# A full-height tile for the low part of q in the attention scores of a four-mixer decoder layer

## The chip, the cores and the metric

The kernel runs on one core of one Trainium2 chip. The metric is the device time of one execution in microseconds (us), start to end. Engines: TensorE (PE, with its weight load shown apart as PEld), VectorE (DVE), ScalarE (ACT), GpSimd (POOL) and SyncE (SP), which issues the DMAs here.

## The reference, cut to what matters

One layer (`DEPTH = 1`) over 1024 tokens of width 1024. After an RMSNorm, one input projection feeds four token mixers; their outputs are normalised per head, gated, concatenated and sent through one output projection. Three of the mixers are causal attentions with 64-wide queries and keys; the fourth (D) is a recurrence.

```python
proj = h @ w_in[l]
...
s = jnp.einsum('bhqcd,bhkcd->bhcqk', qb, k).astype(jnp.float32) * scale + bias[None, :, None]   # A
w = p[:, :, 0] - lam * p[:, :, 1]
...
z = jnp.einsum('bhqd,bhkd->bhqk', qb, k).astype(jnp.float32) * scale                            # B
a = jnp.where(causal, jnp.exp(log_beta + after), 0.0)
...
s = jnp.einsum('bhqd,bhkd->bhqk', qb, k).astype(jnp.float32) * scale                            # C
s = s + (fb[..., :, None] - cum_f[..., None, :])
...
h_res = h_res + mixed @ w_out[l]
```

All of it is in float32, so products that matter are made from operands split in two parts, a high one rounded for the matmul and a low one that holds the rest.

## The kernel before, in words

**Stages.** First the norm, then group D's projections and preparation. Then twelve attention jobs in a row (line 1076): jobs 0 to 3 are pairs of heads of B, jobs 4 to 7 heads of A (two score maps each), jobs 8 to 11 pairs of heads of C. While job i is computed, the projections of job i + 1 and some gate projections are computed too: their matmuls (line 280, in `proj`) stand between the attention matmuls on PE. GpSimd splits every projection weight into `wh` and `wl` (lines 191 and 192 in `load_w`), and, spread over jobs 0 to 3 by a low priority, it inverts group D's triangles (`inv_steps`, lines 855 and 857). After job 11 come group D's chunk chain (`chunk_local`, `chunk_state`, whose matmuls are in `four`, line 968) and the output projection (`out_blocks`, line 931). The output weights are split by `split_w`: seven of the sixteen 128-row blocks early, into tiles that the attention gives back (`split_w_early`), nine later (`split_w_late`).

**Order.** The program is written as one stream; a scheduler puts it into a fixed order on each engine when the kernel is built, and each engine runs its own list in that order. The only fixed order between engines is by semaphores.

**The scores.** Two 64-row heads (or the two maps of one A head) share a job's tiles. `proj_qk` makes from a projection of 128 rows (head 0 on partitions 0 to 63, head 1 on 64 to 127) the tiles `q0`, `q1` and `ql`, one for each half of the tokens, and `k0`, `k1`. In `k0` partitions 0 to 63 hold the high part of head 0's keys and 64 to 127 the low part; in `k1` it is the other way round for head 1. `q0` holds the high part of head 0's queries twice, `q1` that of head 1. `ql` holds the low part of both heads' queries, each on its own 64 partitions. So in `scores` the first matmul gives high times high plus high times low over 128 rows, and the second adds low times high over the 64 rows of its head:

```python
n = h * 64
mm = nc.tensor.matmul(ps[:, :w], lhsT=t[f"q{h}"][qh][:, qs], rhs=t[f"k{h}"][:, c0:c1], start=True, stop=False)
nc.tensor.matmul(ps[:, :w], lhsT=t["ql"][qh][n:n + 64, qs], rhs=t[f"k{h}"][n:n + 64, c0:c1], start=False, stop=not diag)
```

The first is line 397, the second line 401; line 403 adds a mask, in B alone. Each job calls `scores` 24 times, 288 in all. The columns `w` are 128 to 512: a block of 128 queries against the keys up to its own, in chunks of at most 512. In `proj_qk` line 323 makes the low part, `ql` for queries and `kl` for keys. The attention's own tiles lie in the pool `attw`; `q0`, `q1`, `ql` have three buffers each.

Of the kernel before, what the change touches and what calls it, by code (L numbers as in the profile page):

```python
# [10 lines left out]
F32 = mybir.dt.float32  # L11
F32R = mybir.dt.float32r
# [3 lines left out]
ALU = mybir.AluOpType  # L16
# [3 lines left out]
P = 128  # L20
# [3 lines left out]
HS = 512  # L24
# [31 lines left out]
WORDER = (4, 5, 6, 7, 8, 9, 0, 1, 10, 11, 2, 3, 12, 13, 14, 15)  # L56
# [34 lines left out]
def hybrid_trunk_kernel(  # L91
# [23 lines left out]
    nc = tc.nc  # L115
# [3 lines left out]
    def pool(stack, name, bufs=1, space=None, side="left"):  # L119
        kw = {"side": side, "reuse_waits": "tile"} if space is None else {"space": space}  # L120
        return stack.enter_context(tc.tile_pool(name=name, bufs=bufs, **kw))
# [5 lines left out]
    def bank(tag, bufs, name):  # L127
        return psum.tile([P, HS], F32, tag=tag, bufs=bufs, name=name)
# [3 lines left out]
    def rdma(dst, src):  # L132
        nc.sync.dma_start(dst.bitcast(F32), src.bitcast(F32))
# [28 lines left out]

    exp_ln_tables()

# [1 line left out]
    cst = cp.tile([P, C_END], F32, name="cst")  # L166
    def vec(src, n, name, eng=nc.sync):
        t = cp.tile([P, n], F32, name=name)
# [61 lines left out]
    nc.vector.tensor_scalar(qkg[:, 0:1], qkg[:, 0:1], 0.125, None, op0=ALU.mult)  # L230
    nc.vector.tensor_scalar(qkg[:, 2:3], qkg[:, 2:3], 0.125, None, op0=ALU.mult)

# [1 line left out]
    hTh = hpool.tile([P, KT, S], F32R, name="hTh")  # L234
    hTl = hpool.tile([P, KT, S], F32R, name="hTl")

# [6 lines left out]
    with xst:  # L243
# [14 lines left out]
        for hf in range(2):  # L258
            for kt in range(KT):
                ps = bank(("pj", "sc", "mm")[kt % 3] if hf == 0 else ("sc", "mm")[kt % 2], 2, "pst")  # L260
# [4 lines left out]
                split = nc.scalar.activation(dh, ps, AF.Copy, scale=ng[:, kt:kt + 1])  # L265
# [1 line left out]
                    after(split, norms[ACTORD[kt]])  # L267
                nc.vector.scalar_tensor_tensor(dl, ps, ng[:, kt:kt + 1], dh.bitcast(F32), op0=ALU.mult, op1=ALU.subtract)  # L268

# [1 line left out]
    def proj(col, evac, M=P, hold=None, wts=None):  # L271
        wts = load_w(col) if wts is None else wts
        pss = [bank("pj", 2, "pj") for _ in range(2)]
        for hf in range(2):
            cs = slice(hf * HS, (hf + 1) * HS)
            n = 0
            for kt in range(KT):
                wh, wl = wts[kt // 4]
                for a, b in ((wh, hTh), (wh, hTl), (wl, hTh)):
                    mm = nc.tensor.matmul(pss[hf][:M, :], lhsT=a[:, kt % 4, :M], rhs=b[:, kt, cs], start=n == 0, stop=n == 3 * KT - 1)  # L280
                    if n == 0 and hold is not None:
                        after(mm, hold)
                    n += 1
            evac(hf, cs, pss[hf])

# [1 line left out]
    class Att:  # L287
        pass

    at = Att()  # L290
    at.held = []

    def head_rstd(src, sumw, width, sq, ps, table=None):
        nc.scalar.activation(sq, src, AF.Square)
        nc.tensor.matmul(ps, lhsT=sumw, rhs=sq, start=True, stop=True)  # L295
        rstd_from(sq, ps, 1.0 / width, eps, table)
        return sq

    def qk_tiles(pl):
        t = {}  # L300
        for n in ("q0", "q1", "ql"):
            t[n] = [pl.tile([P, HS], F32R, tag=n, bufs=3, name=n) for _ in range(2)]
        for n in ("k0", "k1"):
            t[n] = pl.tile([P, S], F32R, tag=n, bufs=2, name=n)
        return t

    late_qk = dram.tile([4, P, HS], F32, name="late_qk")

    def proj_qk(col, which, t, gain, tmp, late=None):
        def finish_qk(hf, cs, ps, table=None):  # L310
            a0, a1 = t[which + "0"], t[which + "1"]
            if which == "q":
                a0, a1, cs = a0[hf], a1[hf], slice(0, HS)
            low = t["ql"][hf] if which == "q" else tmp.tile([P, HS], F32R, tag="pjl", bufs=1, name="kl")
            if gain is None:
                src, sc = ps, (0.125 if which == "q" else 1.0)
            else:
                src, sc = tmp.tile([P, HS], F32, tag="pjt", bufs=2, name="qn"), 1.0
                rs = head_rstd(ps, blk, 64, src, bank("pn", 1, "psn"), table)
                nc.vector.scalar_tensor_tensor(src, ps, gain, rs, op0=ALU.mult, op1=ALU.mult)  # L320
            nc.scalar.activation(a0[:, cs], src, AF.Copy, scale=sc)
            nc.scalar.activation(a1[:, cs], src, AF.Copy, scale=sc)
            nc.vector.scalar_tensor_tensor(low, src, sc, a0[:, cs].bitcast(F32), op0=ALU.mult, op1=ALU.subtract)
            if which == "q":
                rdma(a0[64:128, cs], a1[0:64, cs])
                rdma(a1[0:64, cs], a1[64:128, cs])
            else:
                rdma(a0[64:128, cs], low[0:64])
                rdma(a1[0:64, cs], low[64:128])

        def evac(hf, cs, ps):
            if late is None:
                finish_qk(hf, cs, ps)
                return
            raw = tmp.tile([P, HS], F32, tag="pjt", bufs=2, name="qr")
            nc.scalar.copy(raw, ps)
            spot = late_qk[2 * (which == "k") + hf]
            nc.sync.dma_start(spot, raw)

            def finish_late(table):  # L340
                src = at.fin.tile([P, HS], F32, tag="gl", bufs=2, name="ql")
                nc.sync.dma_start(src, spot)
                finish_qk(hf, cs, src, table)

            late.append(finish_late)

        proj(col, evac)
# [43 lines left out]
    def scores(t, h, qb, c0, c1, last=None):  # L391
        ps = bank("sc", 2, "sc")
        w = c1 - c0
        qs = slice(qb % 4 * P, qb % 4 * P + P)
        qh = qb // 4
        n = h * 64
        mm = nc.tensor.matmul(ps[:, :w], lhsT=t[f"q{h}"][qh][:, qs], rhs=t[f"k{h}"][:, c0:c1], start=True, stop=False)  # L397
        if at.first is None:
            at.first = mm
        diag = last is not None and c1 == (qb + 1) * P  # L400
        nc.tensor.matmul(ps[:, :w], lhsT=t["ql"][qh][n:n + 64, qs], rhs=t[f"k{h}"][n:n + 64, c0:c1], start=False, stop=not diag)  # L401
        if diag:
            nc.tensor.matmul(ps[:, w - P:w], lhsT=identb, rhs=last, start=False, stop=True)
        return ps
# [41 lines left out]
        nc.gpsimd.tensor_mul(y, y, gt)  # L446
        nc.sync.dma_start(mix[f * P:f * P + P, cs], y)

# [1 line left out]
    def proj_pair_b(p, pl, tmp):  # L450
        t = qk_tiles(pl)
        proj_qk(COL["bq"] + p * P, "q", t, None, tmp)
# [43 lines left out]
        else:  # L496
            finish(ot, f, J, blk, 64, tmp)

# [1 line left out]
    def setup_a(tmp):  # L500
        oht = tmp.tile([NB, OHW], F32, tag="oh", bufs=1, name="oht")
        nc.sync.dma_start(oht, onehot)
# [76 lines left out]
            else:  # L579
                finish(ot, p, J, ones, 128, tmp)  # L580

# [1 line left out]
    at.fbt = cp.tile([72, 1], F32, name="fbt")  # L583
    after(nc.sync.dma_start(at.fbt[64:72, :], forget_bias.rearrange("o h -> h o")), w_dma[-1])
    at.fb = at.fbt[64:72]
# [45 lines left out]
            else:  # L631
                finish(ot, 8 + p, J, blk, 64, tmp)

# [1 line left out]
    rw = Att()  # L635

    def spill(name):
# [201 lines left out]
                nc.scalar.copy(dst[64 * h:64 * h + 64, :, c2, :], src[64 * c2:64 * c2 + 64, :, h, :])  # L839
        keep(rw.rkv, 2, vt)  # L840

# [1 line left out]
    def inv_load(ip):  # L843
        rw.y = ip.tile([P, CH, CH], F32, name="yinv")
        rw.ytmp = ip.tile([P, 512], F32, name="ytmp")
# [14 lines left out]
        for q in range(4):  # L860
            nc.sync.dma_start(rw.abky[:, :, 3, q].rearrange("c (h t) s -> (c h) t s", h=2), rw.y[32 * q:32 * q + 32])

# [1 line left out]
    def split_w(f, opr, wh, wl):  # L864
        raw = opr.tile([P, DM], F32, tag="raw", bufs=2, name="wraw")
        nc.sync.dma_start(raw, w_out[0, f * P:(f + 1) * P, :])
# [14 lines left out]
    def wide(pl, tag, name):  # L881
        return [pl.tile([P, DM], F32R, tag=tag, bufs=2, name=name)]

    def thin(pl, tags, name):
        return [pl.tile([P, HS], F32R, tag=t, bufs=3, name=name) for t in tags]

    def split_w_early(pl, opr, wo):
        def vs_pair(f):
            t = pl.tile([P, 2, DM], F32R, tag="vs", bufs=2, name=f"wo{f}")
            return [t[:, 0]], [t[:, 1]]  # L890

        spots = [lambda f: vs_pair(f),
                 lambda f: (wide(pl, "k0", f"woh{f}"), wide(pl, "k1", f"wol{f}")),
                 lambda f: (thin(pl, ("q0", "q1"), f"woh{f}"), thin(pl, ("ql", "q0"), f"wol{f}")),
                 lambda f: (thin(pl, ("q1", "ql"), f"woh{f}"), thin(pl, ("q0", "q1"), f"wol{f}")),
                 lambda f: (wide(pl, "k0", f"woh{f}"), wide(pl, "k1", f"wol{f}")),
                 lambda f: (wide(pl, "bt", f"woh{f}"), wide(pl, "bt", f"wol{f}")),
                 lambda f: vs_pair(f)]
        for f, spot in zip(WORDER, spots):
            wh, wl = spot(f)  # L900
            split_w(f, opr, wh, wl)
            wo[f] = halves(wh, wl)

    def split_w_late(op, opr, wo):
        for f in WORDER[7:]:
            wh = [op.tile([P, DM], F32R, name=f"woh{f}")]
            wl = [op.tile([P, DM], F32R, name=f"wol{f}")]
            split_w(f, opr, wh, wl)
            wo[f] = halves(wh, wl)
# [151 lines left out]
            op(y3, y3, b)  # L1061
        nc.sync.dma_start(mix[12 * P:16 * P, ts_].rearrange("(q p) t -> p q t", p=P), y3)

# [1 line left out]
    with ExitStack() as st:  # L1065
        dp0 = pool(st, "dp0", 1)
        dp = pool(st, "dp", 1)
# [11 lines left out]
    at.fin = pool(ctx, "fin", 1)  # L1079
    with ExitStack() as st:  # L1080
        pl = pool(st, "attw", 1)
        late_pools = st.enter_context(ExitStack())
        pp = pool(late_pools, "attp", 1)
        tmp = pool(late_pools, "attt", 1)
# [58 lines left out]
        pair = out_blocks(0, 2, wo)  # L1143
# [49 lines left out]
```

## Time and profile before

| what | value |
|---|---|
| time, median of 3 runs | 1626.15 us (1625.5 to 1627.73) |
| profiled execution, span | 1628.0 us |
| PE busy | 1555.1 us, 96% |
| PEld busy | 1183.9 us, 73% |
| DVE busy | 978.7 us, 60% |
| POOL busy | 906.2 us, 56% |
| ACT busy | 744.3 us, 46% |

The profile shows one execution; its own time is known by its span. A PE matmul's bar runs to the end of its modelled pipeline, so bars of neighbours overlap, and the rate of the engine is read from start to start. "Idle before, releaser" names what ended an engine's idle time; "issue" is time in which it waited for nothing that the profile shows. Shapes are partitions x elements; for a matmul the first pair (as 64*128) is that of the stationary operand.

### The profile page before, as it was taken

The page shows a single profiled execution, that of the slowest core. Times are in us where ns is not written, and L with a number is a line of the kernel's source. Part 1 is how long each engine was busy: PE and PEld are TensorE (multiplying, and loading weights), DVE is VectorE, ACT ScalarE, POOL GpSimd, SP SyncE. Part 2 cuts the span into 40 slices and gives each one's busy share as a digit, 9 for nine tenths or more (in the row PEclk, how much of TensorE's full clock was granted, in tenths as well). Part 3 has the DMA queues.
Part 4 walks back from the last instruction along what each step waited for, and adds up shares of the span by engine and source line. Part 5 has one row for each costly group of instructions (what it writes and reads, how often), then busy time and mean ns, then how long its engine had stood idle before and what let it go on. Part 6 is the DMA issues. An engine that isn't in the chain of part 4 may idle for free.

```text
span 1628.0 us, 23497 instructions
## 1 busy us (share of the span) xinstructions
PE 1555.1 (96%) x8180; PEld 1183.9 (73%) x8180; DVE 978.7 (60%) x1739; ACT 744.3 (46%) x1601; POOL 906.2 (56%) x992
## 2 busy tenths in 40 slices
PE   6899999999989899899999999999999999999999
PEld 4777777767667676576777777777777678788887
DVE  6677763776998888466556544453456774544321
ACT  5534433443444445545556555565566654311110
POOL 3566755999999998133323356757576744300000
PEclk9999999999999999999999999999999999999999
DMA  6454567212222222622322233323227456755232
GB/s 159 102 132 102 132 163 200 59 43 71 56 62 56 78 78 57 170 52 59 98 71 72 78 91 111 97 79 111 84 84 187 120 135 165 210 140 130 82 104 65
DMA packets 259758, 168.76 MB, mean 104 GB/s; under 512 B 127948, under 2 KB 222412, under 8 KB 259512
## 3 DMA queue, kind: packets, MB, share of 16 engines
q1 hardware_dynamic: 259640, 167.26, 39.1%
q8 instruction: 65, 1.06, 0.3%
q14 instruction: 53, 0.43, 0.1%
HBM read 107.40 MB, written 49.60 MB: 96 GB/s over the span
## 4 chain that ended last, share of the span: by engine, by line
PE 64%; POOL 16%; DVE 7%; issue 6%; ACT 3%; DMA 3%; SPq 1%; POOLq 0%; DVEq 0%; ACTq 0%
PE pj L280 27%; PE pso L931 10%; POOL yinv L857 5%; POOL ytmp L855 5%; PE sc L401 5%; PE psf L968 4%; PE pt L417 3%; PE sc L397 3%; PE psn L295 3%; POOL wl L192 2%; PE po L427 2%; PE po L426 1%; POOL wh L191 1%; DMA wraw<-in_w_out_dram 1%; POOL sh L682 1%
## 5 line engine op out<-in xcount | busy, mean ns | idle before, releaser
L280 PE MATMUL pj<-hTh,wh 128*128 128x512 f32 (+1 forms) x1040 | 424.8, 409 | 14.6 <-POOL wh L191 7.2
L280 PE MATMUL pj<-hTh,wl 128*128 128x512 f32 (+1 forms) x1040 | 419.0, 407 | 12.5 <-POOL wl L192 12.1
L280 PE MATMUL pj<-hTl,wh 128*128 128x512 f32 (+1 forms) x1040 | 415.8, 400 | 0.3 <-DVE hTl L268 0.3
L280 PEld LDWEIGHTS pj<-hTh,wh 128*128 128x128 f32 (+1 forms) x1040 | 198.2, 191 | 69.7 <-issue 17.9
L280 PEld LDWEIGHTS pj<-hTh,wl 128*128 128x128 f32 (+1 forms) x1040 | 197.8, 190 | 66.6 <-POOL wl L192 17.0
L280 PEld LDWEIGHTS pj<-hTl,wh 128*128 128x128 f32 (+1 forms) x1040 | 198.0, 190 | 44.0 <-issue 5.4
L192 POOL TENSOR_TENSOR wl<-raw,wh 128x512 fp32r<-128x512 f32 (+1 forms) x130 | 185.5, 1427 | 10.5 <-PE pj L280 4.9
L191 POOL TENSOR_SCALAR wh<-raw 128x512 fp32r<-128x512 f32 (+1 forms) x130 | 100.0, 769 | 155.5 <-PE pj L280 137.7
L421 DVE TENSOR_TENSOR ptl<-pt,pth 128x512 fp32r<-128x512 f32 x240 | 126.4, 549 | 68.0 <-ACT pth L420 67.5
L420 ACT CAST pth<-pt 128x512 fp32r<-128x512 f32 x240 | 109.0, 481 | 126.8 <-PE pt L417 107.5
L475 DVE TENSOR_TENSOR_SCAN qs<-qs 128x128 f32<-128x128 f32 (+3 forms) x96 | 136.6, 1429 | 11.3 <-ACT qs L138 11.3
L553 ACT ACTIVATE Pt<-Pt,st 128x512 f32<-128x512 f32 (+2 forms) x192 | 116.8, 611 | 53.5 <-DVE st L548 52.7
L857 POOL TENSOR_TENSOR yinv<-yinv,ytmp 128x486 f32<-128x486 f32 (+44 forms) x106 | 127.3, 1201 | 4.0
L401 PE MATMUL sc<-k,ql 64*128 64x512 f32 (+3 forms) x288 | 127.6, 443 | 0.0
L855 POOL TENSOR_TENSOR ytmp<-yinv 128x486 f32<-128x486 f32 (+44 forms) x106 | 120.6, 1137 | 8.4 <-DMA raw<-in_w_in_dram 4.3
L477 DVE TENSOR_TENSOR Pt<-Pt,qs 128x128 f32<-128x128 f32 (+3 forms) x96 | 102.3, 1072 | 35.0 <-POOL qs L474 19.1
L417 PE MATMUL pt<-cst,Pt 128*128 128x128 f32 x720 | 118.0, 276 | 3.8 <-DVE Pt L477 3.8
L397 PE MATMUL sc<-k,q 128*128 128x512 f32 (+3 forms) x288 | 116.1, 403 | 2.1 <-DVE st L548 1.1
L1061 POOL TENSOR_TENSOR yc<-yc,lbg 128x512 f32<-128x512 f32 x16 | 21.2, 1325 | 150.7 <-DVE yc L1055 150.3
L417 PEld LDWEIGHTS pt<-cst,Pt 128*128 128x128 f32 x720 | 86.5, 141 | 23.3 <-issue 5.6
L401 PEld LDWEIGHTS sc<-k,ql 64*128 64x128 f32 x288 | 53.1, 185 | 68.0 <-issue 61.3
L613 POOL TENSOR_SCALAR bt<-cb,cumq 128x128 f32<-128x128 f32 (+3 forms) x64 | 52.9, 828 | 70.3 <-DVE st L548 67.8
(254 smaller groups left out, 2961.4 us busy)
## 6 DMA issues: line engine op xcount, KB each, us to landing
raw<-in_w_in_dram SPq DMA_DIRECT2D x128, 256.0 KB, 3.0
cb<-cum SPq DMA_DIRECT2D x16, 512.0 KB, 4.0
bd<-abky SPq DMA_DIRECT2D x32, 256.0 KB, 5.7
wraw<-in_w_out_dram SPq DMA_DIRECT2D x16, 512.0 KB, 4.0
om<-mix SPq DMA_DIRECT2D x32, 256.0 KB, 3.1
q<-q SPq DMA_DIRECT2D x48, 128.0 KB, 2.2
k<-kl SPq DMA_DIRECT2D x48, 128.0 KB, 2.3
gl<-gates SPq DMA_DIRECT2D x24, 256.0 KB, 3.0
```

Of the source, the lines that this page charges most:

```text
L191: nc.gpsimd.tensor_scalar(wh[:, :, :M], raw[:, :, :M], 1.0, 0.0, op0=ALU.mult, op1=ALU.add)
L192: nc.gpsimd.tensor_sub(wl[:, :, :M], raw[:, :, :M], wh[:, :, :M].bitcast(F32))
L280: mm = nc.tensor.matmul(pss[hf][:M, :], lhsT=a[:, kt % 4, :M], rhs=b[:, kt, cs], start=n == 0, stop=n == 3 * KT - 1)
L397: mm = nc.tensor.matmul(ps[:, :w], lhsT=t[f"q{h}"][qh][:, qs], rhs=t[f"k{h}"][:, c0:c1], start=True, stop=False)
L401: nc.tensor.matmul(ps[:, :w], lhsT=t["ql"][qh][n:n + 64, qs], rhs=t[f"k{h}"][n:n + 64, c0:c1], start=False, stop=not diag)
L417: nc.tensor.transpose(pt[:, (b - a) * P:(b - a + 1) * P], ptiles[b][kb // 4][:, kb % 4 * P:(kb % 4 + 1) * P], ident)
L421: nc.vector.tensor_sub(pl[:, :n], pt[:, :n], ph[:, :n].bitcast(F32))
L475: nc.vector.tensor_tensor_scan(q[:, :w][:, ::-1], q[:, :w][:, ::-1], q[:, :w][:, ::-1], 1.0 if after is None else after, op0=ALU.mult, op1 ...
L553: nc.scalar.activation(et[:, :w], et[:, :w], AF.Exp, scale=-1.0, bias=init, accum_out=st[:, 2 + i:3 + i])
L855: nc.gpsimd.tensor_mul(t, y[:, a:a + n, r:r + 1].to_broadcast([P, n, r]), y[:, r:r + 1, :r].to_broadcast([P, n, r]))
L857: nc.gpsimd.tensor_add(y[:, a:a + n, :r], y[:, a:a + n, :r], t)
L931: mm = nc.tensor.matmul(ps[b][half], lhsT=l, rhs=r[half], start=n == 0, stop=n == 47)
```

## The change

`ql` is replaced by two tiles per half of the tokens, `l0` and `l1`, one for each head. Each has 128 partitions; the 64 of the other head hold zeros, and the second score matmul reads all 128 rows of the low tile and of `k0` or `k1`. The tiles are made once, three for each head, and their zero halves are set once (`low_tiles`, called where `attw` is opened); the jobs take them in rotation. The low part is now made by two subtractions on 64 partitions in place of one on 128. Since the tag `ql` now has six buffers, the early split of the output weights takes eight blocks and the late one eight. The diff also removes some comment lines, left out here.

```diff
     def qk_tiles(pl):
         t = {}
-        for n in ("q0", "q1", "ql"):
+        for n in ("q0", "q1"):
             t[n] = [pl.tile([P, HS], F32R, tag=n, bufs=3, name=n) for _ in range(2)]
+        for h in range(2):
+            t[f"l{h}"] = [at.low[h][(at.units + J) % 3] for J in range(2)]
+        at.units += 2
...
+    def low_tiles(pl):
+        at.units = 0
+        at.low = [[], []]
+        for h in range(2):
+            other = slice(64 - 64 * h, 128 - 64 * h)
+            for _ in range(3):
+                t = pl.tile([P, HS], F32R, tag="ql", bufs=6, name=f"ql{h}")
+                nc.gpsimd.memset(t[other].bitcast(F32), 0.0)
+                at.low[h].append(t)
...
-            low = t["ql"][hf] if which == "q" else tmp.tile([P, HS], F32R, tag="pjl", bufs=1, name="kl")
+            if which == "k":
+                low = tmp.tile([P, HS], F32R, tag="pjl", bufs=1, name="kl")
...
-            nc.vector.scalar_tensor_tensor(low, src, sc, a0[:, cs].bitcast(F32), op0=ALU.mult, op1=ALU.subtract)
             if which == "q":
+                for h in range(2):
+                    hs = slice(64 * h, 64 * h + 64)
+                    nc.vector.scalar_tensor_tensor(t[f"l{h}"][hf][hs], src[hs], sc, (a0, a1)[h][hs, cs].bitcast(F32),
+                                                   op0=ALU.mult, op1=ALU.subtract)
                 rdma(a0[64:128, cs], a1[0:64, cs])
                 rdma(a1[0:64, cs], a1[64:128, cs])
             else:
+                nc.vector.scalar_tensor_tensor(low, src, sc, a0[:, cs].bitcast(F32), op0=ALU.mult, op1=ALU.subtract)
...
-        n = h * 64
...
-        nc.tensor.matmul(ps[:, :w], lhsT=t["ql"][qh][n:n + 64, qs], rhs=t[f"k{h}"][n:n + 64, c0:c1], start=False, stop=not diag)
+        nc.tensor.matmul(ps[:, :w], lhsT=t[f"l{h}"][qh][:, qs], rhs=t[f"k{h}"][:, c0:c1], start=False, stop=not diag)
...
-        return [pl.tile([P, HS], F32R, tag=t, bufs=3, name=name) for t in tags]
+        return [pl.tile([P, HS], F32R, tag=t, bufs=6 if t == "ql" else 3, name=name) for t in tags]
...
-                 lambda f: (thin(pl, ("q0", "q1"), f"woh{f}"), thin(pl, ("ql", "q0"), f"wol{f}")),
-                 lambda f: (thin(pl, ("q1", "ql"), f"woh{f}"), thin(pl, ("q0", "q1"), f"wol{f}")),
+                 lambda f: (thin(pl, ("q0", "q1"), f"woh{f}"), thin(pl, ("ql", "ql"), f"wol{f}")),
+                 lambda f: (thin(pl, ("q0", "q1"), f"woh{f}"), thin(pl, ("ql", "ql"), f"wol{f}")),
+                 lambda f: (thin(pl, ("q0", "q1"), f"woh{f}"), thin(pl, ("ql", "ql"), f"wol{f}")),
...
-        for f in WORDER[7:]:
+        for f in WORDER[8:]:
...
         pl = pool(st, "attw", 1)
+        low_tiles(pl)
```

**PE, job 4 (head 0 of A), second half of its tokens, scores of one block of queries.** `sc` are scores, `pj` projections, `po` the product with the values, `pt` transposes. Before:

```order
L280 MATMUL pj<-hTl,wh 128x512
L280 MATMUL pj<-hTh,wl 128x512
L397 MATMUL sc<-k_5733,q_5729 128x512
L401 MATMUL sc<-k_5733,ql 128x512
L397 MATMUL sc<-k_5733,q_5729 128x256
L401 MATMUL sc<-k_5733,ql 128x256
L280 MATMUL pj<-hTh,wh 128x512
L280 MATMUL pj<-hTl,wh 128x512
```

With the change (lines 397 and 401 are now 414 and 418):

```order
L280 MATMUL pj<-hTh,wl 128x512
L446 MATMUL po<-pth,vs 128x512
L414 MATMUL sc<-k_5743,q_5741 128x512
L418 MATMUL sc<-k_5743,ql_2400 128x512
L447 MATMUL po<-ptl,vs 128x512
L448 MATMUL po<-pth,vs 128x512
```

Each pair of score matmuls still stands together; what stands before and after it shifts by some places.

**DVE, the low part of a query projection for job 5.** Before:

```order
L556 RECIPROCAL st<-st 128x1
L323 SCALAR_TENSOR_TENSOR ql<-qn,q_6463 128x512
L568 SCALAR_TENSOR_TENSOR Pt<-Pt,st 128x512
L320 SCALAR_TENSOR_TENSOR qn<-pj,qkg,qn 128x512
L555 TENSOR_TENSOR st<-st 128x1
```

With the change:

```order
L585 SCALAR_TENSOR_TENSOR Pt<-Pt,st 128x512
L340 SCALAR_TENSOR_TENSOR ql_2398<-qn,q_6475 64x512
L340 SCALAR_TENSOR_TENSOR ql_2404<-qn,q_6477 64x512
L572 TENSOR_TENSOR st<-st 128x1
L573 RECIPROCAL st<-st 128x1
```

One instruction on 128 partitions has become two on 64, one behind the other.

**POOL, the end of group D's preparation, with the change.** `wh` and `wl` are split projection weights, `ytmp` the first step of the inversion:

```order
L191 TENSOR_SCALAR wh<-raw 128x512
L192 TENSOR_TENSOR wl<-raw,wh 128x512
L317 MEMSET ql_2394 64x512
L317 MEMSET ql_2396 64x512
L317 MEMSET ql_2398 64x512
L317 MEMSET ql_2400 64x512
L317 MEMSET ql_2402 64x512
L317 MEMSET ql_2404 64x512
L489 MEMSET qs 128x1
```

The six memsets are new; before, the memset of `qs` (line 472 there) stood right behind that `wl`.

## Rows read from the trace of the kernel before

**Rows 1.** Page, part 1: busy time of each engine, share of the span.

```profile
PE 1555.1 (96%) x8180; PEld 1183.9 (73%) x8180; DVE 978.7 (60%) x1739; ACT 744.3 (46%) x1601; POOL 906.2 (56%) x992
```

**Rows 2.** Busy time by stretch; columns as in the first line.

```profile
core 0: us, PE busy (x) PEld busy (x) DVE busy (x) ACT busy (x) POOL busy (x), PEclk, DMA share, GB/s
283.00:650.00 367.00, 343.82 (x1558) 255.23 (x1559) 301.09 (x324) 165.26 (x362) 351.24 (x377) 0.96 0.23 62
677.00:1250.00 573.00, 568.72 (x2464) 412.92 (x2463) 303.92 (x811) 325.01 (x745) 286.92 (x359) 0.99 0.33 90
1250.00:1330.00 80.00, 78.01 (x603) 58.20 (x603) 59.72 (x149) 47.69 (x116) 49.66 (x67) 1.00 0.46 120
1330.00:1400.00 70.00, 64.69 (x580) 53.82 (x578) 38.27 (x57) 31.09 (x53) 38.33 (x22) 0.98 0.70 197
1400.00:1628.00 228.00, 224.02 (x1573) 188.41 (x1572) 78.97 (x140) 36.59 (x69) 16.36 (x13) 1.00 0.41 110
```

**Rows 3.** Timeline of PE in job 4: start us, us, instruction.

```profile
703.27 0.39 PE L280 MATMUL pj<-hTh,wh 128*128 128x512 f32 x1
703.50 0.39 PE L280 MATMUL pj<-hTl,wh 128*128 128x512 f32 x1
...
703.95 0.39 PE L397 MATMUL sc<-k,q 128*128 128x512 f32 x1
704.27 0.50 PE L401 MATMUL sc<-k,ql 64*128 64x512 f32 x1
704.70 0.38 PE L397 MATMUL sc<-k,q 128*128 128x256 f32 x1
705.01 0.38 PE L401 MATMUL sc<-k,ql 64*128 64x256 f32 x1
705.32 0.50 PE L280 MATMUL pj<-hTh,wh 128*128 128x512 f32 x1
705.65 0.39 PE L280 MATMUL pj<-hTl,wh 128*128 128x512 f32 x1
```

**Rows 4.** Timeline of PE in job 8.

```profile
1028.71 0.40 PE L397 MATMUL sc<-k,q 128*128 128x512 f32 x1
1029.04 0.50 PE L401 MATMUL sc<-k,ql 64*128 64x512 f32 x1
1029.47 0.51 PE L280 MATMUL pj<-hTh,wh 128*128 128x512 f32 x1
1029.81 0.40 PE L280 MATMUL pj<-hTl,wh 128*128 128x512 f32 x1
1030.05 0.28 PE L427 MATMUL po<-ptl,vs 128*128 128x256 f32 x1
1030.16 0.23 PE L426 MATMUL po<-pth,vs 128*128 128x128 f32 x1
```

**Rows 5.** Line 401 in 677 to 1250 us: its weight loads and its matmuls.

```profile
L401 PEld LDWEIGHTS sc<-k,ql x167: 182/183/285, 678.0 to 1249.4; 64*128 64x128 f32 x167
L401 PE MATMUL sc<-k,ql x167: 323/490/789, 678.0 to 1249.4; 64*128 64x512 f32 x83, 64*128 64x128 f32 x28, 64*128 64x256 f32 x28, 64*128 64x384 f32 x28
...
  issue: 38.1, 131
```

**Rows 6.** Weight loads of line 280, 677 to 1250 us.

```profile
L280 PEld LDWEIGHTS pj<-hTh,wh 128*128 128x128 f32 x448 | 84.5, 189 | 24.5 <-issue 7.0 <-POOL bt L614 0.5 <-POOL Pt L565 0.5
```

**Rows 7.** Waits of PE, 677 to 1250 us, longest first: total us, times, longest.

```profile
PE po L427 <- DVE ptl L421: 1.2, 1, 1.2
```

**Rows 8.** Waits of DVE, 677 to 1250 us.

```profile
DVE Pt L548 <- PE sc L401: 75.0, 69, 4.3
DVE ptl L421 <- ACT pth L420: 42.1, 24, 4.7
DVE st L555 <- ACT Pt L553: 41.1, 39, 2.5
DVE Pt L548 <- PE pt L417: 36.5, 17, 5.8
```

**Rows 9.** Waits of DVE for PE, 1250 to 1330 us, the longest.

```profile
DVE Pt L548 <- PE sc L401: 4.3, 5, 1.9
```

**Rows 10.** Waits of POOL, 283 to 650 us, all of them.

```profile
POOL qs L472 <- DVE Pt L477: 2.5, 3, 1.7
POOL qs L474 <- DVE qs L475: 2.3, 3, 1.1
```

**Rows 11.** DVE groups by form: the low part of q, and a 64-partition operation.

```profile
L323 DVE SCALAR_TENSOR_TENSOR ql<-qn,q 128x512 fp32r<-128x512 f32 x16 | 12.3, 770 | 7.9 <-ACT q L321 7.9
...
L437 DVE TENSOR_TENSOR ot<-po,oc 64x512 f32<-64x512 f32 x32 | 21.8, 681 | 15.4 <-ACT oc L436 14.9
```

**Rows 12.** Timeline of POOL where the memsets come to stand.

```profile
260.56 0.10 POOL L472 MEMSET qs<- 128x1 f32 x1
268.17 0.62 POOL L191 TENSOR_SCALAR wh<-raw 128x512 fp32r<-128x512 f32 x1 [7.50 <-PE pj L280]
```

**Rows 13.** POOL groups by form: a long memset.

```profile
L951 POOL MEMSET bd<- 128x2048 f32 x2 | 3.8, 1878 | 5.2 <-PE pj L280 5.2
```

**Rows 14.** Chain that ended last, in order of time: a late output weight.

```profile
1362.18 5.75 DMA wraw<-in_w_out_dram
...
1367.95 1.06 ACT woh L869
1369.08 2.41 POOL wol L870
```

## The prediction

> **What bounds the kernel now.** I read the page's first part first: PE is busy for 96% of the span and no other engine for more than 73% [rows 1], but bars of matmuls overlap, and an average over stages says nothing of any of them. So I read the busy times by stretch, cut at the jobs [rows 2]. There are three kinds of stage in which scores are computed. In 283 to 650 us (jobs 0 to 3, B) POOL is busy for 351.24 of 367.00 us, and it waits there for nobody but DVE, 2.5 + 2.3 us in all [rows 2, 10]: POOL sets the length of this stage. In 677 to 1250 us (jobs 4 to 10, A and most of C) PE is busy for 568.72 of 573.00 us, and its longest wait of all is 1.2 us [rows 2, 7], while DVE, ACT and POOL stand at 303.92, 325.01 and 286.92 us [rows 2]: PE sets the length. In 1250 to 1330 us (job 11 beside group D's chunk chain) PE shows 78.01 of 80.00 and DVE 59.72 [rows 2]; both matter. After that come no scores.
>
> Then I read PE from start to start. Between two neighbouring projection matmuls of 512 columns lie 0.23 us (703.27 to 703.50) [rows 3]. One of 256 columns is followed after 0.11 us (1030.05 to 1030.16) [rows 4], and for 384 columns I take 0.17, three quarters of 0.23. A score pair does not keep this pace. In rows 3 the first of a pair of 512 columns is followed by its low part after 0.32 us, the low part by the next matmul after 0.43, and in the pair of 256 columns the steps are 0.31 and 0.31, then 0.33 to the second projection. In rows 4 the three steps around a pair of 512 are 0.33, 0.43, 0.34.
>
> What differs is the 64*128 form of line 401. Its weight load, 183 ns, waits: 38.1 us in 131 of 167 cases by "issue", that is for no semaphore [rows 5]. The loads of line 280 take 189 ns and come at a pace of 0.23 us per matmul, so they lie under the matmul before [rows 3, 6]. I read this as the engine emptying itself when it goes from matmuls of 128 rows to one of 64, and once more on the way back, with the next weight load caught behind it.
>
> **The change, part by part.**
>
> *The row form of the low matmul.* Columns and counts stay; the same number of columns over 128 rows should take the pace of line 280. The extra of a pair is what its steps exceed that pace by:
> - 512 columns in rows 3: 0.32 - 0.23 and 0.43 - 0.23, sum 0.29 (the step after is that of the next pair);
> - 256 columns in rows 3: 0.31 - 0.11, 0.31 - 0.11, 0.33 - 0.23, sum 0.50;
> - 512 columns in rows 4: 0.33 - 0.23, 0.43 - 0.23, 0.34 - 0.23, sum 0.41.
>
> The mean of the three is 0.40 us. It is spent 167 times in 677 to 1250 us [rows 5], 67 us in all. There are 24 pairs for each of twelve jobs: 96 of them lie in B, 38 us, and the 25 that are left (288 - 96 - 167) lie in job 11, 10 us.
>
> *What of it shortens the run.* In 677 to 1250 us there is no other engine to hide it, so the bounds are 0 and 67. What comes next is the path of a softmax through DVE and ACT, whose waits PE now has time to cover. DVE waits there for PE for 75.0 + 36.5 = 111.5 us [rows 8]; a PE that is 67 us faster takes away part of that wait and leaves DVE some 45 us of it. Its other large waits, for ACT, are 42.1 + 41.1 us [rows 8]. So the engines behind PE can follow, though not at every block: each engine keeps its fixed order, and transposes now come sooner after the scores that they need. I take 60 of 67. In 1250 to 1330 us DVE is busy for 75% and its longest wait for PE is 4.3 us [rows 2, 9]: I take 5 of 10. In B, POOL's list does not get shorter and what could come free on it is 4.8 us at most [rows 10]: bounds 0 and 5, I take 2. Sum: 67 us.
>
> *DVE.* 24 query halves get a second subtraction. One on 128 partitions takes 770 ns, and an operation on 64 partitions of the same 512 columns takes 681, hardly less [rows 11]; so two cost about twice one, and 24 times 0.7 to 0.77 is 17 to 18 us of DVE. Two thirds of it fall into A and C, where DVE is idle for 573.00 - 303.92 = 269 us [rows 2]; a third, some 6 us, into B, where DVE is busy for 301.09 of 367.00 us. Behind it wait the release of the projection's `pj` bank and the copies that duplicate q. Taken at nothing; without the cover it is 17 us, kept below as a rival.
>
> *POOL.* Six memsets of 64x512. Between 100 ns for one column [rows 12] and 1878 ns for 2048 columns [rows 13], 512 columns lie near 0.54 us, so 3.3 us in all. They wait for nothing but POOL's own work and stand where POOL was idle for 7.50 us, waiting for PE [rows 12]: nothing. Were that gap gone, 3.3 us would come on top, since B begins right behind it.
>
> *The output weights.* One of nine late blocks moves to the early ones. A late block costs a load of 5.75, a copy of 1.06 and a subtraction of 2.41 us one behind the other [rows 14], overlapped with its neighbours through two buffers, so it is worth up to half of 9.2, some 4 us. But its early tile is given back only when job 11's last scores are done, so it may as well be late there: bounds -4 and +4, I take 0. From 1400 us on PE is busy for 224.02 of 228.00 us with work that stays [rows 2].
>
> The sum: 67 us less than the profiled 1628.0, which is 0.1% above the median of the runs. Against the median of 1626.15 it is 1559; I say **1560 us**.
>
> **Rivals.**
>
> *The gap belongs to the pair, not to the rows (slower).* If the second matmul waited because it adds to the bank that the first still writes, 128 rows would keep every gap. Then only the added work is left: while DVE makes two low parts, a `pj` bank stays taken for 0.7 us more, PE's next projection waits for it, 24 times, and the time is 1626 + 17 = 1643. It decides where DVE's second subtraction ends after PE wants the bank again; if the bank is free in time, nothing changes. Against it: the projections of line 280 add to one bank in a row, at 0.23 us [rows 3]. I give it 0.06, two thirds of that for slower.
>
> *The load stays exposed.* If the zero-padded tile's weight load could not run under the matmul before it, the step into the low matmul would keep its extra: 0.09, 0.20 and 0.10 in the three pairs, mean 0.13 of 0.40. The gain would be two thirds of that above, 45 us, and the time 1581. Against it: line 280's loads of 189 ns at a pace of 0.23 us [rows 3, 6]. I give it 0.04. The Trainium skill has a rule for this rival, in "TensorE: Matmul & The Clock Gate", section "Part 3: Packing small matmuls — row/col tiling": weight loads overlap matmuls in flight only when the row group differs, and full-height tiles share all of theirs. The same section also allows a load into a background buffer, and the trace sides with that second sentence: 189 ns under 0.23 us.
>
> *The softmax chain takes most of it back.* If the blocks' waits for DVE and ACT come to the front in A and C, half or less of the 67 us is won: gains of 15 to 35, a time near 1601. For it: DVE waits 83 us for ACT there [rows 8], and none of that shrinks. Against it: PE waits for next to nothing now [rows 7], and DVE has 111.5 us of waiting for PE to lose. I give it 0.08.
>
> *B gains too.* If POOL's bars in B hold waiting for its partners, B would shrink by its 38 us as well: 1523. For it only that the spans of POOL are rough. I give it 0.04.
>
> **How the numbers follow.** The forecast, a gain between 36 and 94 us, has 0.78; the rivals in order 0.06, 0.04, 0.08 and 0.04. The top of the gain is 67 + 10 + 5 + 4 = 86, and 8 more if the pairs that I priced were cheap ones: 0.45 in place of 0.40 on 167 pairs. The bottom is half of 67 with little from job 11. So the range is 1532 to 1590; it takes in the exposed load too. A measurement of this kernel tells about 0.2%, 3 us, from no change. Faster: 0.78 + 0.04 + 0.08 + 0.04 = 0.94; same 0.02 and slower 0.04, both from the first rival.
>
> **What would show it.** In the profile after, the low matmuls stand in the form 128*128, and from the first of a pair of 512 columns to the second and on to the next are 0.23 us each. The stretch of jobs 4 to 10 is about 60 us shorter with PE still without waits; B keeps its 367 us and POOL its 95%; the time from job 11's end to the end stays. The forecast is wrong if the step into the low matmul stays above 0.3 us, if PE in jobs 4 to 10 shows waits of over 30 us for DVE or ACT, or if B shrinks by more than 10 us.

## The result and the profile after

The changed kernel takes **1562.22 us** (median of 4 runs, 1561.54 to 1562.86) against 1626.26 us of the kernel before in the same comparison: ratio 0.9599, 95% interval 0.9587 to 0.961. The forecast was 1560 us, between 1532 and 1590. The profiled execution has a span of 1560.3 us, 67.7 less than before.

The stages, from the first start and the last end of line 397 (414 after) in each job of both traces, in us:

| stage | before | after | difference | forecast |
|---|---|---|---|---|
| job 0's first score to job 4's first (B and the way out of it) | 283.0 to 677.8 | 287.2 to 677.3 | job 4 comes 0.5 earlier | -2 |
| job 4's first score to job 11's first (A, most of C) | 677.8 to 1253.0 | 677.3 to 1190.1 | -62.4 | -60 |
| job 11 | 1253.0 to 1327.8 | 1190.1 to 1258.6 | -6.3 | -5 |
| from there to the end | 300.2 | 301.7 | +1.5 | 0 |

Job 0's first score itself comes 4.2 us later than before, job 1's comes at 374.9 and at 375.2 us; so the first row is read by where job 4 begins.

The first part of the page, of the kernel after, answers to [rows 1]:

```profile
PE 1465.9 (94%) x8180; PEld 1180.1 (76%) x8180; DVE 999.8 (64%) x1763; ACT 739.8 (47%) x1602; POOL 911.6 (58%) x999
```

PE's bars are 89 us shorter in sum; DVE has 24 instructions more. The busy times by stretch, cut at the same jobs (the last two in another place than in rows 2), answer to [rows 2] (columns as there):

```profile
283.00:650.00 367.00, 323.30 (x1570) 255.79 (x1570) 303.62 (x330) 162.25 (x362) 352.94 (x378) 0.96 0.23 63
677.00:1188.00 511.00, 504.82 (x2453) 408.06 (x2452) 317.50 (x822) 324.02 (x745) 288.04 (x359) 1.00 0.35 99
1188.00:1260.00 72.00, 69.17 (x586) 55.46 (x585) 57.80 (x148) 46.03 (x112) 52.07 (x70) 1.00 0.54 143
1260.00:1333.00 73.00, 68.61 (x549) 55.83 (x547) 39.62 (x62) 34.53 (x60) 36.41 (x20) 1.00 0.68 191
1333.00:1560.00 227.00, 223.25 (x1641) 188.48 (x1639) 80.74 (x141) 34.86 (x66) 15.65 (x12) 1.00 0.41 109
```

In B, POOL is as busy as before and PE 20 us less; in 677 to 1188 us PE does in 511 us nearly what took 573. The timeline of PE in job 4 shows why, and answers to [rows 3]:

```profile
699.74 0.39 PE L446 MATMUL po<-pth,vs 128*128 128x512 f32 x1
699.97 0.39 PE L414 MATMUL sc<-k,q 128*128 128x512 f32 x1
700.20 0.39 PE L418 MATMUL sc<-k,ql 128*128 128x512 f32 x1
700.42 0.39 PE L447 MATMUL po<-ptl,vs 128*128 128x512 f32 x1
...
701.73 0.28 PE L414 MATMUL sc<-k,q 128*128 128x256 f32 x1
701.84 0.28 PE L418 MATMUL sc<-k,ql 128*128 128x256 f32 x1
701.96 0.34 PE L447 MATMUL po<-ptl,vs 128*128 128x384 f32 x1
```

Three steps of 0.23, 0.23 and 0.22 us at 512 columns, and 0.11 and 0.12 at 256: a score pair now keeps the pace of line 280. The view of line 418 (the low matmul, 401 before) in 677 to 1188 us, to be laid beside [rows 5]:

```profile
L418 PEld LDWEIGHTS sc<-k,ql x168: 187/188/192, 677.4 to 1187.6; 128*128 128x128 f32 x168
...
  issue: 2.9, 12
```

The load is 188 ns where it was 183, but it stands idle by "issue" for 2.9 us in 12 cases where it was 38.1 in 131: it lies under the matmul before. The waits of PE in the same stretch, the three longest:

```profile
PE sc L414 <- DVE st L565: 2.2, 4, 0.8
PE pj L280 <- DVE qn L334: 1.5, 4, 0.6
PE po L444 <- DVE ptl L438: 1.2, 1, 1.2
```

Hardly more than before [rows 7]: PE still sets the length of A and C. The waits of DVE there, to be compared with [rows 8]:

```profile
DVE st L572 <- ACT Pt L570: 42.3, 42, 2.0
DVE Pt L565 <- PE sc L418: 32.6, 39, 2.7
DVE Pt L565 <- PE pt L434: 32.2, 14, 5.3
...
DVE ptl L438 <- ACT pth L437: 10.2, 16, 1.9
```

DVE's two waits for PE fell from 111.5 to 64.8 us. Of its two large waits for ACT one stayed (41.1 before, 42.3 after), and the other, that of `ptl` for `pth`, fell from 42.1 to 10.2 us. And in B, the waits of PE for POOL in 283 to 650 us, before:

```profile
PE pj L280 <- POOL wl L192: 10.9, 9, 2.0
PE pj L280 <- POOL wh L191: 6.8, 3, 3.2
...
PE pj L280 <- POOL qs L472: 1.0, 2, 0.7
```

And after:

```profile
PE pj L280 <- POOL wl L192: 17.5, 14, 2.6
PE pj L280 <- POOL wh L191: 15.6, 10, 4.7
PE pj L280 <- POOL qs L489: 4.9, 4, 2.3
```

They are 38.0 us in sum where they were 18.7: there the time that the pairs gave back has become idle time.

### The profile page after: what moved, and what is told of

Same layout as the page of the kernel before. It is cut to its first block, busy times and chain, and to the rows that moved or that the text cites. A ratio compares the mean times of both kernels' runs of the same rounds, so it can differ in the third digit from the quotient of the medians.

```text
span 1560.3 us, 23517 instructions
## 1 busy us (share of the span) xinstructions
PE 1465.9 (94%) x8180; PEld 1180.1 (76%) x8180; DVE 999.8 (64%) x1763; ACT 739.8 (47%) x1602; POOL 911.6 (58%) x999
## 4 chain that ended last, share of the span: by engine, by line
PE 58%; POOL 20%; DVE 8%; issue 6%; ACT 3%; DMA 2%; SPq 1%; POOLq 0%; DVEq 0%; ACTq 0%
PE pj L280 25%; PE pso L949 10%; POOL yinv L874 7%; POOL ytmp L872 6%; PE psf L986 5%; POOL wl L192 3%; PE pt L434 3%; PE psn L295 3%; PE sc L414 2%; PE sc L418 2%; PE po L444 1%; PE po L443 1%; DMA wraw<-in_w_out_dram 1%; POOL wh L191 1%; POOL sh L699 1%
## 5 line engine op out<-in xcount | busy, mean ns | idle before, releaser
L492 DVE TENSOR_TENSOR_SCAN qs<-qs 128x128 f32<-128x128 f32 (+3 forms) x96 | 135.3, 1413 | 10.9 <-ACT qs L138 10.7
L414 PE MATMUL sc<-k,q 128*128 128x512 f32 (+3 forms) x288 | 111.8, 389 | 3.7 <-DVE st L565 3.0
L418 PE MATMUL sc<-k,ql 128*128 128x512 f32 (+3 forms) x288 | 99.3, 349 | 0.0
L138 ACT ACTIVATE qs<-sc 128x128 f32<-128x128 f32 (+3 forms) x96 | 47.8, 498 | 89.9 <-DVE qs L492 42.5
L949 PE MATMUL pso<-wol,omh 128*128 128x512 f32 x224 | 89.1, 398 | 0.0
```

Of the source, the lines that this page charges most:

```text
L418: nc.tensor.matmul(ps[:, :w], lhsT=t[f"l{h}"][qh][:, qs], rhs=t[f"k{h}"][:, c0:c1], start=False, stop=not diag)
L492: nc.vector.tensor_tensor_scan(q[:, :w][:, ::-1], q[:, :w][:, ::-1], q[:, :w][:, ::-1], 1.0 if after is None else after, op0=ALU.mult, op1 ...
L949: mm = nc.tensor.matmul(ps[b][half], lhsT=l, rhs=r[half], start=n == 0, stop=n == 47)
```

## The experiments

The theory: PE pays some 0.40 us for each detour from 128-row matmuls to one of 64 rows and back, and it is worth time only where PE sets the length, in A, C and job 11. Rivals: the gain came from something else in the change; the pairs of B have a share.

### 64 rows again, everything else as changed

```diff
-        nc.tensor.matmul(ps[:, :w], lhsT=t[f"l{h}"][qh][:, qs], rhs=t[f"k{h}"][:, c0:c1], start=False, stop=not diag)
+        hs = slice(64 * h, 64 * h + 64) if True else slice(0, P)
+        nc.tensor.matmul(ps[:, :w], lhsT=t[f"l{h}"][qh][hs, qs], rhs=t[f"k{h}"][hs, c0:c1], start=False, stop=not diag)
```

> The change with the second score matmul on the 64 rows of its head again; the tiles with zeros, the two subtractions on DVE, the memsets and the eight early weight blocks stay, and so does the order on every engine. Theory (emptying the engine at each change between 128 and 64 rows, 0.40 us for a pair): the whole gain goes, 1620 to 1632 us, and the steps around a low matmul of 512 columns are 0.32, 0.43 and 0.34 us again. Rival (the gain came from the order, the weight blocks or the split of the subtraction): it stays at 1562 us.

1626.09 us, ratio 0.9986 (0.9975 to 0.9997) to the kernel before. Its PE timeline in job 4, with the 64-row form (line 419 here):

```profile
708.93 0.39 PE L280 MATMUL pj<-hTh,wl 128*128 128x512 f32 x1
709.16 0.39 PE L414 MATMUL sc<-k,q 128*128 128x512 f32 x1
709.48 0.50 PE L419 MATMUL sc<-k,ql 64*128 64x512 f32 x1
709.91 0.38 PE L447 MATMUL po<-pth,vs 128*128 128x256 f32 x1
710.13 0.28 PE L448 MATMUL po<-ptl,vs 128*128 128x256 f32 x1
```

The steps are 0.32 and 0.43 again, and the 256 columns that follow take 0.22 in place of 0.11. All 8180 matmuls of this trace stand in the order that they have after the change, so the two can be laid side by side. Around the 168 low matmuls of jobs 4 to 10 the step in is longer by 0.11 us in the mean, the step out by 0.15 and the next step by 0.08 (where no other pair follows): 56 us in sum, 0.33 us a pair. The medians, for pairs that no other pair follows, are 0.40, 0.39 and 0.39 us at 512, 384 and 256 columns, and 0.29 at 128. A pair of 512 that another pair follows costs 0.29, since the step behind it is the other's step in.

So the row form, with the order of the instructions and all the rest held still, is worth 64 us; the rest of the change (two subtractions, memsets, one more early block) is worth at most a quarter of a per cent. The first theory stands, its first rival falls.

### 64 rows in one group of jobs only

The same line with `hs = slice(64 * h, 64 * h + 64) if last is not None else slice(0, P)` (64 rows in B, which alone passes a mask), and with `last is None` (64 rows in A and C).

> The change with 64 rows in B (jobs 0 to 3) alone, 128 rows in A and C. Theory (POOL sets the length of B): same as the change, 1560 to 1565 us, B from 287 to 646 us as there. Rival (B wins a share by its 96 pairs): 1570 us or more, B longer by over 8 us.

> The change with 64 rows in A and C and 128 rows in B alone. Theory: no gain left, 1621 to 1630 us. Rival (each pair is worth the same wherever it stands): a third of 64 us remains, 1605 us.

64 rows in B: 1562.75 us (0.9599, 0.9574 to 0.9623), the time of the change. 64 rows in A and C: 1626.65 us (0.9988, 0.9975 to 1.0001), the time before. The 96 pairs of B are worth nothing, the 192 others all of it. The busy times of B in the two kernels, 64 rows and then 128 rows in B:

```profile
283.00:650.00 367.00, 341.60 (x1559) 253.22 (x1559) 301.52 (x328) 163.18 (x360) 352.05 (x378) 0.97 0.24 63
```

```profile
283.00:650.00 367.00, 321.63 (x1572) 254.14 (x1571) 304.36 (x330) 162.75 (x363) 352.38 (x377) 0.96 0.24 63
```

PE differs by 20 us, POOL's 352 us do not, and job 4 begins at 677.2 and at 676.6 us.

### Two 64-row matmuls behind one another

In the kernel before, the low matmul in two halves of its columns:

```diff
-        nc.tensor.matmul(ps[:, :w], lhsT=t["ql"][qh][n:n + 64, qs], rhs=t[f"k{h}"][n:n + 64, c0:c1], start=False, stop=not diag)
+        u = w // 2
+        for u0, u1 in ((0, u), (u, w)):
+            nc.tensor.matmul(ps[:, u0:u1], lhsT=t["ql"][qh][n:n + 64, qs], rhs=t[f"k{h}"][n:n + 64, c0 + u0:c0 + u1], start=False, stop=not diag and u1 == w)
```

> The kernel before, with each low matmul cut into two halves of its columns, both on 64 rows, one behind the other with the same weights. Theory (the price is paid where the row form changes, not by each 64-row matmul): the step between the two halves of a 512-column low matmul is that of 256 columns, 0.11 to 0.13 us, and the way out costs 0.20 us over the columns once; the time rises by 12 us at most, 1626 to 1638 us. Rival (each 64-row matmul has its weight load exposed): the step between the halves is 0.2 us longer, 0.3 us, and 192 of these in A and C make 1660 us or more.

One run, 1647.05 us; in its comparison the kernel before took 1627.77. That lies between the times of theory and rival, 9 us above the theory's, so the time tells nothing, all the less as the fixed order on the engines shifted. The steps do. The view merges the two halves of a pair into one line (line 403 here, x2):

```profile
593.18 0.47 PE L397 MATMUL sc<-k,q 128*128 128x512 f32 x1
593.58 0.50 PE L403 MATMUL sc<-k,ql 64*128 64x256 f32 x2
594.01 0.50 PE L280 MATMUL pj<-hTh,wl 128*128 128x512 f32 x1
594.35 0.40 PE L280 MATMUL pj<-hTh,wh 128*128 128x512 f32 x1
```

From the first half to the matmul after both lie 0.43 us, as from the one piece in [rows 4], and the step after is 0.34 again: at 512 columns in all the second 64-row matmul costs nothing. But the split of these 0.43 us is not the one I expected. From the starts in the trace, the median of 138 steps between halves of 256 columns is 0.223 us, not 0.11 to 0.13, and of 150 steps out of the second half 0.207. For halves of 64, 128 and 192 columns the steps between them are 0.133, 0.164 and 0.194 (46 or fewer each), the steps out 0.20. The weight loads decide between theory and rival. In the trace the second half's load starts 0.107 us after the first half, at each of the four widths, and the second half's matmul 0.026, 0.057, 0.087 and 0.116 us behind its load, for halves of 64 to 256 columns. So it waits for the columns of the first half and not for its own load, and the rival falls. The price is paid for the detour, as the theory has it, with its parts in other places than expected; but a second 64-row matmul that is short does cost something, 0.08 us for halves of 64 columns (0.34 in all, where one piece of 128 columns takes a median of 0.254).

### What holds B

B gave back nothing, so two edits took work from POOL there. First, ScalarE makes the high part of the projection weights in jobs 0 to 3:

```diff
+            if wh_act[0]:
+                nc.scalar.copy(wh[:, :, :M], raw[:, :, :M])
+            else:
+                nc.gpsimd.tensor_scalar(wh[:, :, :M], raw[:, :, :M], 1.0, 0.0, op0=ALU.mult, op1=ALU.add)
-            nc.gpsimd.tensor_scalar(wh[:, :, :M], raw[:, :, :M], 1.0, 0.0, op0=ALU.mult, op1=ALU.add)
```

> The change, and in jobs 0 to 3 ScalarE instead of GpSimd makes the high part of the projection weights (some 36 operations of about 1.0 us there leave POOL's list, some 0.5 us each go to ACT, which is busy for 44% of B). Theory (POOL sets the length of B, and the change has left PE time in hand there): 20 to 35 us less than the change, 1527 to 1542 us, all of it in B. Rival (DVE, at 83% there, or the latency between engines bounds B as much): less than 8 us, 1554 us or more.

1552.65 us (0.953, 0.9508 to 0.9553), 10 less than the change: between the two expectations. Job 3 ends at 642.9 us instead of 645.8; what was won lies in the way out of B, where job 4 begins at 666.4 instead of 677.3. POOL now waits for DVE (283 to 640 us), which it hardly did:

```profile
POOL qs L495 <- DVE qs L496: 11.5, 6, 3.4
POOL qs L493 <- DVE qs L496: 6.3, 4, 1.9
```

These are operations of one column on POOL in the midst of DVE's scan of a block. In the kernel after the change DVE waits for them in turn (line 491 copies, 489 sets), 283 to 646 us:

```profile
DVE Pt L494 <- POOL qs L491: 17.1, 9, 4.5
DVE Pt L494 <- POOL qs L489: 13.5, 10, 2.5
```

So the second edit lets DVE make them itself, in the change alone, with the first edit, and both in the kernel before:

```diff
-                nc.gpsimd.memset(q[:, w:w + 1], 1.0)
+                nc.vector.memset(q[:, w:w + 1], 1.0)
...
-                nc.gpsimd.tensor_copy(q[:, w:w + 1], after)
+                nc.vector.tensor_copy(q[:, w:w + 1], after)
```

> The change, and in B the one-column memsets and copies of qs (64 and 32) are made by DVE instead of GpSimd. Theory now (in B, POOL and DVE hold each other: DVE waits 31 us for these little operations, which stand in POOL's queue behind long ones): B is shorter by 8 to 18 us, 1544 to 1554 us. Rival (POOL's own work alone sets B): less POOL work by 17 us and no more, but DVE's work grows by some 9 us; if DVE is the bound, no gain or a loss, 1560 to 1570 us.

> The change with both: wh by ScalarE in jobs 0 to 3 and the little qs operations on DVE. Theory (two engines that hold each other in B; both have to give): 20 to 35 us less than the change, 1527 to 1542 us, more than the two alone in sum. Rival (DVE's own work sets B, 301 us and the 9 more): under 15 us, 1547 us or more.

> The kernel before with the same two edits, 64-row low matmuls as before. Theory (B hides the switches of its 96 pairs behind POOL and DVE only as long as these set its length): the difference to the change with both edits is more than the 64 us of the change itself, 70 to 85 us, 1605 to 1620 us. Rival (B never depends on PE): the difference stays 62 to 66 us.

The second edit alone: 1563.97 us (0.9601, 0.9586 to 0.9615), nothing, as the rival had it, though not for its reason: job 3 ends 9.0 us earlier, at 636.8, and job 4 begins at 677.7 all the same; the gain is given back on the way out of B. Both: 1547.59 us (0.9498, 0.948 to 0.9515), 15 less than the change and more than the two alone in sum (10 less and 2 more), but short of the 20 to 35 expected and just within the rival's bound. Both in the kernel before: 1615.13 us (0.9916, 0.9901 to 0.9932). The difference of the change on this base is 67.5 us, between the two expectations and within the intervals of the 64 us. In the two traces job 3 ends at 639.9 and 637.0 us and job 4 begins at 663.6 and 662.2, so B has begun to depend on PE by 1 to 3 us at most. The kernel with the change and both edits shows, in 283 to 637 us:

```profile
283.00:637.00 354.00, 316.11 (x1567) 251.36 (x1566) 304.07 (x417) 176.47 (x390) 317.16 (x250) 0.97 0.27 72
```

POOL has 37 us in hand, and job 3 ends only 8.8 us earlier than after the change (637.0 instead of 645.8). DVE's longest waits there are

```profile
DVE ptl L442 <- ACT pth L441: 15.2, 6, 5.0
DVE ot L458 <- ACT oc L457: 12.5, 6, 4.3
DVE qs L496 <- ACT qs L138: 8.7, 5, 4.2
DVE kl L349 <- ACT k L340: 5.0, 1, 5.0
DVE vs L384 <- ACT vs L383: 4.3, 1, 4.3
```

Together with 304.07 us of work they make 350 of 354 us. That does not show that DVE holds B: an engine's work and its waits fill any stretch, and for PE, with waits of 37.9 us, the same sum is 354.0. The list shows only that DVE now waits for ACT, where it waited for POOL without the edits. What holds B once POOL has less to do stays open.

### The way out of B

Between job 3's end and job 4's first score lie 31.5 us after the change. There the four stores of the inverted triangles take 10 us of SP's queue, from 642.4 us on, and the loads that job 4 waits for stand behind them (the first of `ql` from `late_qk` at 658.0). Both kernels were run with these stores put behind job 5's first score:

```diff
-            nc.sync.dma_start(rw.abky[:, :, 3, q].rearrange("c (h t) s -> (c h) t s", h=2), rw.y[32 * q:32 * q + 32])
+            after(nc.sync.dma_start(rw.abky[:, :, 3, q].rearrange("c (h t) s -> (c h) t s", h=2), rw.y[32 * q:32 * q + 32]), at.job5)
```

> The kernel with the change, wh by ScalarE and the little qs operations on DVE, and the four stores of the inverted triangles (10 us of the SP queue) put behind job 5's first score instead of right behind the last inversion. Theory (the stores hold up SP's queue, and with it the weight loads and the reload of job 4's projections, just where B ends): 4 to 12 us less than without the move, 1536 to 1544 us. Rival (the end of B hangs on the latency of the norm of job 4's projections alone): within 2 us of 1547.6.

> The change with the same move of the stores alone. Theory: job 4's first score comes 6 to 10 us earlier, 1552 to 1557 us. Rival: the same as the change, 1560 to 1564 us.

With both edits 1545.37 us (0.9492, 0.9473 to 0.951), without them 1559.95 (0.9577, 0.9554 to 0.96): some 2 us each, inside the intervals. In the second, job 4 does begin 3.7 us earlier, at 673.6 us, and job 11 ends at 1258.9 as before: what came early was lost again. The stores were not the main thing. The version with the change and all three edits is the fastest that was run, some 17 us below the change.

Not tried: the early split of seven blocks with the new tiles. The run with 64 rows bounds what the eighth is worth only together with the rest of the change.

## Why the prediction was right, point by point

**The price of a pair.** I took 0.40 us by three pairs, 67 us for the 167 of jobs 4 to 10, and 60 of that as won. The mechanism was right: the run with 64 rows takes the whole gain back. The price was too high. Laid beside that run, the pairs gave back 0.33 us in the mean, 56 us in sum; none of my three pairs had 128 columns, which cost 0.29 by the median. And the discount for what could not follow was hardly needed: from job 4's first score to job 11's the kernel is 58.6 us shorter than with 64 rows, and 62.4 shorter than before. The two errors cancel, so that the 60 came so close is in part luck.

**Who can follow.** I expected DVE to lose part of its 111.5 us of waiting for PE and no new waits in front of PE. It lost 46.7 us, and PE's waits stayed at a few us. The rival of the softmax chain fell. Its argument that none of DVE's 83 us of waiting for ACT would shrink was wrong too: 52.5 of them are left (42.3 and 10.2).

**Job 11** gave 6.3 us where I took 5, **the end** lost 1.5 where I took 0 within 4. Job 11 has 24 pairs and not 25 (the other one is job 10's last, behind 1250 us), and the 4.3 us of rows 9 are the sum of five waits, the longest 1.9.

**B.** The forecast of nearly nothing was right: PE does not set B, as the runs with 64 rows in one group show. That POOL sets it is shown less well. "POOL sets the length of this stage" was read from POOL's 351 us of 367 and its short waits. In the trace after, POOL is idle for only 7 us between its first inversion step, at 277.4 us, and the end of the last, at 642.4. But with some 32 us of weight splitting taken from it (the first edit) the inversions end 31 us earlier, at 611.7, and job 4 begins only 10.9 us earlier; with the second edit alone they end 6.3 us earlier and job 4 begins no earlier. So something else seems to need nearly as long as POOL's list; which, stays open. I had looked for an engine without waits, and had not asked what comes next when it has less to do.

**DVE's second subtraction.** Expected to cost as much as the first, 17 to 18 us in all, and to be hidden. The two lines of the kernel after, beside [rows 11]:

```profile
L340 DVE SCALAR_TENSOR_TENSOR ql<-qn,q 64x512 fp32r<-64x512 f32 x32 | 25.6, 800 | 7.8 <-ACT q L335 6.5 <-ACT q L336 0.9
...
L340 DVE SCALAR_TENSOR_TENSOR ql<-pj,q 64x512 fp32r<-64x512 f32 x16 | 11.0, 686 | 9.2 <-ACT q L336 9.0
```

On 64 partitions it takes 800 and 686 ns; the first form took 770 on 128 [rows 11]. All 48 take 36.6 us where the 24 before took 17.8 (12.3 of it in rows 11), so 18.8 us came on top. It was hidden: the rest of the change costs nothing that the 64-row run could show.

**POOL's memsets.** Expected 3.3 us inside a gap of 7.50. In the timeline of POOL after:

```profile
260.68 2.96 POOL L317 MEMSET ql<- 64x512 f32 x6
...
268.18 0.62 POOL L191 TENSOR_SCALAR wh<-raw 128x512 fp32r<-128x512 f32 x1 [4.49 <-PE pj L280]
```

2.96 us, and the next operation starts at 268.18 as it did at 268.17 [rows 12].

**The other rivals.** The step into the low matmul is 0.23 us, so neither does the gap belong to the pair nor does the load stay exposed; and job 4 came 0.5 us earlier, so B gained nothing. With the exposed load falls what hung on the rule of the Trainium skill, "TensorE: Matmul & The Clock Gate", section "Part 3: Packing small matmuls — row/col tiling", that loads overlap only across row groups: here 128-row loads of 188 ns run under 128-row matmuls. Another page of the Trainium skill, "TensorEngine Tiling (Array Packing)", section "Key Properties", states that changing the tiling mode drains the engine. The prediction's reading of the gaps fits that; the page gives no time for it, and here the way there and back costs 0.29 to 0.40 us. The emptying itself is argued from the steps; no view here shows it.

## What to carry to other kernels

A single matmul on 64 rows among matmuls on 128 is dearer than the same columns on 128 rows with zeros: by 0.29 us at 128 columns and 0.40 at 512 in these traces, read from start to start, since bars hide it. It is worth that only where PE sets the length, so cut the count by stages first: a third of the 288 pairs were worth nothing. Price a change by all forms that it touches, not by a few that catch the eye. And an engine that is busy for 96% of a stage need not hold it by much: taking some 32 us from it here gave 10.

## What the runs showed of the hardware that was not expected

**96 rows are no detour.** The kernel before has matmuls on 96 rows in group D's preparation. Its PE timeline:

```profile
172.22 0.40 PE L280 MATMUL pj<-hTh,wl 128*128 128x512 f32 x1
172.46 0.39 PE L760 MATMUL psz<-lo,up 96*128 96x512 f32 x1
172.69 0.39 PE L280 MATMUL pj<-hTh,wh 128*128 128x512 f32 x1
172.92 0.40 PE L280 MATMUL pj<-hTl,wh 128*128 128x512 f32 x1
```

Steps of 0.24, 0.23 and 0.23 us: the pace of 128 rows, in and out. Whether 65 rows would do is not shown.

**The detour's parts.** In a single 64-row matmul of 512 columns the extra is 0.09 to 0.10 us on the way in, 0.20 on the way out and 0.10 to 0.11 at the step after [rows 3, 4]. With two in a row the 0.20 splits into some 0.11 between them and 0.10 behind the second (0.223 - 0.11 and 0.207 - 0.11), so a second 64-row matmul of 256 columns adds nothing. Why the parts lie so was not settled.
